# Forming the low half of each weight block by an accumulating DMA

## The chip, the cores and the metric

The kernel runs on one core of one Trainium2 chip. The metric is the device time of one execution in microseconds (us). Before the change it is 972.54 us, the median of three runs (970.15 to 978.56).

## What is computed

Two layers act on x, 512 rows of 1024 float32 numbers. Each is x + rmsnorm(mixer(rmsnorm(x))). The even layer has one input projection, which feeds an S5 state-space branch and a convolution branch, and one output projection. The odd layer is a chunked gated linear attention (GLA) with four heads. Cut to the parts that matter here:

```python
u = rms_norm(x, norm_pre[0]);  p = u @ ev_w_in[0]
a_in, a_z, b_val, b_gate, b_z = split(p)
ya = gelu(s5_layer(a_in, ...))                       # 64 groups, 64 complex states each
ya = ya * sigmoid(ya @ s5_w_glu + s5_b_glu) * silu(a_z)
yb = silu(layer_norm(causal_depthwise_conv31(b_val * sigmoid(b_gate)))) @ conv_w_pw * silu(b_z)
x = x + rms_norm(concat(ya, yb) @ ev_w_out[0], norm_post[0])
u = rms_norm(x, norm_pre[1]);  q, k, v, r, lr = split(u @ od_w_in[0])
y = rms_norm(gla_chunked(q, k, v, log_sigmoid(lr @ w_gate_up + b) / 16)) * silu(r)
x = x + rms_norm(y @ od_w_out[0], norm_post[1])
```

## The kernel before

**Two halves of every matrix.** TensorE (PE) multiplies in a rounded 32-bit format (fp32r). To keep float32 accuracy, activations and weights are each split in two: a high half, which is the rounded value, and a low half, which is the value less the rounded one. A product is the sum of three matmuls: high weight by high activation, high weight by low activation, low weight by high activation.

**136 weight blocks in a row.** All weights form one list (`wlist`, L87 to L112) of blocks of 128 x 1024 numbers, 512 KB each: 40 of the input projection, 8 of the GLU, 8 of the S5 half of the output projection, 8 of the pointwise projection, 8 of the convolution half, then for each of four heads 12 blocks (queries and keys, values, gate), with 8 blocks of the second output projection after the heads 2 and 3. `w_raw` (L115) starts the load of a block into one of three `wraw` buffers from SyncE's (SP's) DMA queue. `w_split` (L124) turns it into `wh` and `wl`, with two buffers each: ScalarE (ACT) makes the rounded copy at L138, and VectorE (DVE) or GpSimd (POOL) subtracts it from the raw block at L140. The set `pool_split` (L151) gives 45 blocks to POOL and leaves the rest to DVE. `w_get` (L156) hands over the next block and splits the one after it. The instructions of `w_split` are recorded under `feed()` (L145), a higher priority for the scheduler. Ten blocks are split into resident tiles instead, `hres`/`lres` at the end of each output projection (L865 to L868) and `wres` (L940); these are not split ahead.

**How a block is used.** `mm_st` (L170) uses the weights as the stationary operand: 16 matmuls with `wh` (L175, L176), then 8 with `wl` (L178). It serves 72 blocks. `mm_mv` (L765) streams the weights as the moving operand, and L773, L774 (with `wh`) and L775 (with `wl`) take turns, so that `wl` is needed from the first matmuls on. It serves the 32 blocks of values and gates and the 32 of the output projections; ten of these 64 are the resident ones.

**What else is in the queues.** While the 40 blocks of the input projection are multiplied, the S5 branch runs for eight channel tiles c: `s5_prep` makes tables (DVE and POOL), `s5_in` a scan over blocks of time (L563 to L589, mostly DVE), `s5_out` the outputs (PE). The convolution (`conv`, L622) has 31 taps of 128x512 for each tile, the first on ACT (L625) and 30 on DVE (L628, L629), recorded under `background()`, a low priority. After it come GLU, layer norm and the two halves of the output projection; then the heads of layer 1. A scheduler orders the instructions of each engine when the kernel is built, and each engine then runs its own queue in that order and waits at the head of it. The DMA instructions of an engine stand in the same queue.

## Time and profile before

| | |
|---|---|
| runs | 970.15, 972.54, 978.56 us |
| profiled execution: span from first to last instruction | 977.0 us, 4.5 us (0.5%) above the median; what the execution takes outside its span is shown by no view |
| PE busy | 910.5 us (93%) |
| DVE busy | 722.4 us (74%), over 98% of the time from 50 to 400 us |
| ACT busy | 430.9 us (44%) |
| POOL busy | 403.9 us (41%), most of it before 250 us |
| DMA | 109.17 MB, all issued from SP; its queue took 32.8% of the sixteen engines |
| PE clock, mean over the span | 0.978 of full |

In the lines of the profile, L140 is line 140 of the kernel before; `x12` counts instructions; "busy, mean ns" is their time together and of one; "idle before <-releaser" is what the engine waited for ahead of them. In a table of windows each engine has its busy time in the stretch and in brackets its instructions, PEclk is the clock that PE was granted, and "DMA share" is the mean busy share of the sixteen DMA engines. A chain shows the work that ended last, step by step.

### The profile page before, as it was taken

Reading aid. Unit: us, or ns where it says so; the run is one execution under the profiler, and the core shown is the slowest. Engines: PE = TensorE matmul, PEld = TensorE weight load, DVE = VectorE, ACT = ScalarE, POOL = GpSimd, SP = SyncE. Lnnn points to the kernel's source line nnn. Section 1 sums busy time; section 2 is a strip of 40 time slices with the busy share of each in tenths; the row PEclk is TensorE's granted clock in tenths of the full one; section 3 lists DMA queues with packets and bytes.
Section 4 is the critical chain, followed back from the end, with each engine's and each line's share of the span. In section 5 each row is a group of like instructions: output and inputs, shape, how many; then the busy total and the mean of one; then the engine's idle time right before and its main releaser. Section 6 shows DMA issues by size and latency. Waiting matters only on the chain.

```text
span 977.0 us, 11973 instructions
## 1 busy us (share of the span) xinstructions
PE 910.5 (93%) x4396; PEld 726.1 (74%) x4396; DVE 722.4 (74%) x1210; ACT 430.9 (44%) x646; POOL 403.9 (41%) x335
## 2 busy tenths in 40 slices
PE   4978998699799999999999898999999999999996
PEld 3866776476577777777888676788888888888875
DVE  7999999999999999894457758857374322563546
ACT  5313566565454843454244465434353342342431
POOL 3499999999833594751126203100020020000212
PEclk9998999889899999999999999999999999999998
DMA  6333423334324433415244311311212123323612
GB/s 216 130 102 110 144 65 121 101 100 121 100 79 140 162 112 126 161 66 172 87 162 155 136 58 50 130 66 65 82 70 87 65 87 129 129 83 138 232 44 86
DMA packets 44330, 109.17 MB, mean 112 GB/s; under 512 B 12849, under 2 KB 14385, under 8 KB 44273
## 3 DMA queue, kind: packets, MB, share of 16 engines
q1 hardware_dynamic: 44272, 108.42, 32.8%
q8 instruction: 34, 0.56, 0.2%
q14 instruction: 24, 0.19, 0.1%
HBM read 95.18 MB, written 13.22 MB: 111 GB/s over the span
## 4 chain that ended last, share of the span: by engine, by line
PE 51%; DVE 25%; ACT 4%; issue 2%; DMA 1%; POOL 0%; DVEq 0%; SPq 0%; ACTq 0%; POOLq 0%
DVE ps_cv L628 8%; PE ps_mm L773 8%; PE ps_mm L775 8%; PE ps_mm L774 8%; PE ps_mm L178 6%; PE ps_mm L175 6%; PE ps_mm L176 6%; PE ps_aux L1035 2%; DVE zb L580 1%; DVE cme L484 1%; DVE cme L488 1%; PE ps_mm L880 1%; PE ps_mm L876 1%; PE ps_mm L877 1%; DVE bcum L955 1%
## 5 line engine op out<-in xcount | busy, mean ns | idle before, releaser
L138 ACT CAST wh<-wraw 128x1024 fp32r<-128x1024 f32 x125 | 131.3, 1050 | 177.2 <-PE ps_mm L774 81.1
L140 DVE TENSOR_TENSOR wl<-wraw,wh 128x1024 fp32r<-128x1024 f32 x82 | 108.1, 1319 | 101.2 <-ACT wh L138 99.4
L628 DVE SCALAR_TENSOR_TENSOR ps_cv<-h,cw,ps_cv 128x512 f32<-128x512 f32 x232 | 162.0, 746 | 1.9 <-ACT ps_cv L625 0.9
L140 POOL TENSOR_TENSOR wl<-wraw,wh 128x1024 fp32r<-128x1024 f32 x44 | 112.1, 2548 | 106.4 <-ACT wh L138 61.0
L175 PE MATMUL ps_mm<-u0h,wh 128*128 128x512 f32 x320 | 133.3, 417 | 8.4 <-ACT tmp L652 8.4
L176 PE MATMUL ps_mm<-u0l,wh 128*128 128x512 f32 x320 | 130.8, 409 | 0.0
L773 PE MATMUL ps_mm<-wh,u1h 128*128 128x512 f32 x240 | 95.1, 397 | 0.2 <-DVE bcum L948 0.2
L774 PE MATMUL ps_mm<-wh,u1l 128*128 128x512 f32 x240 | 94.8, 395 | 0.0
L775 PE MATMUL ps_mm<-wl,u1h 128*128 128x512 f32 x240 | 90.7, 395 | 0.0
L178 PE MATMUL ps_mm<-u0h,wl 128*128 128x512 f32 x320 | 85.1, 403 | 5.2 <-DVE wl L140 5.2
L175 PEld LDWEIGHTS ps_mm<-u0h,wh 128*128 128x128 f32 x320 | 63.1, 197 | 26.6 <-ACT tmp L652 10.1
L178 PEld LDWEIGHTS ps_mm<-u0h,wl 128*128 128x128 f32 x320 | 59.8, 191 | 20.6 <-DVE wl L140 6.1
L176 PEld LDWEIGHTS ps_mm<-u0l,wh 128*128 128x128 f32 x320 | 62.9, 197 | 14.5 <-issue 1.0
L935 POOL TENSOR_TENSOR rg<-rg,ng 128x512 f32<-128x512 f32 x16 | 25.5, 1626 | 114.8 <-ACT rg L934 114.8
L1021 POOL TENSOR_TENSOR kr<-kr,fac 128x384 f32<-128x384 f32 x8 | 8.4, 1044 | 136.9 <-DVE rs_y L189 77.7
L773 PEld LDWEIGHTS ps_mm<-wh,u1h 128*128 128x128 f32 x240 | 45.2, 188 | 10.7 <-DVE bcum L948 0.5
L774 PEld LDWEIGHTS ps_mm<-wh,u1l 128*128 128x128 f32 x240 | 45.2, 188 | 10.0
L775 PEld LDWEIGHTS ps_mm<-wl,u1h 128*128 128x128 f32 x240 | 45.0, 188 | 10.2
L176 PE MATMUL ps_mm<-u1l,wh 128*128 128x512 f32 x128 | 50.7, 396 | 0.0
L175 PE MATMUL ps_mm<-u1h,wh 128*128 128x512 f32 x128 | 50.6, 395 | 0.0
L178 PE MATMUL ps_mm<-u1h,wl 128*128 128x512 f32 x128 | 35.1, 412 | 3.4 <-DVE wl L140 3.4
L773 PE MATMUL ps_mm<-wh,oth 128*128 128x512 f32 x96 | 38.0, 397 | 0.1
(356 smaller groups left out, 2134.3 us busy)
## 6 DMA issues: line engine op xcount, KB each, us to landing
wraw<-in_w_in_dram SPq DMA_DIRECT2D x40, 512.0 KB, 3.3
wraw<-in_w_out_dram SPq DMA_DIRECT2D x32, 512.0 KB, 3.3
wraw<-in_w_vr_dram SPq DMA_DIRECT2D x32, 512.0 KB, 3.2
wraw<-in_w_qk_dram SPq DMA_DIRECT2D x16, 512.0 KB, 3.2
tm<-kt_d SPq DMA_DIRECT2D x8, 512.0 KB, 4.6
wraw<-in_w_glu_dram SPq DMA_DIRECT2D x8, 512.0 KB, 3.6
wraw<-in_w_pw_dram SPq DMA_DIRECT2D x8, 512.0 KB, 3.2
x<-in_x_dram SPq DMA_DIRECT2D x4, 512.0 KB, 5.2
```

What stands on the lines that cost most here:

```text
L138: SC.copy(h, raw)
L140: eng.tensor_tensor(out=l, in0=raw, in1=h.bitcast(F32), op=ALU.subtract)
L175: PE.matmul(acc, whv[:, k, :], xh[:, k, :], start=(k == 0), stop=False)
L176: PE.matmul(acc, whv[:, k, :], xl[:, k, :], start=False, stop=False)
L178: PE.matmul(acc, wlv[:, k, :], xh[:, k, :], start=False, stop=(k == KT - 1))
L484: eng.tensor_tensor(out=o, in0=pr[:, 0, hg, lo:lo + TB].unsqueeze(pa).to_broadcast(sh), in1=m1.unsqueeze(5 - pa).to_broadcast(sh), op=ALU. ...
L628: V.scalar_tensor_tensor(out=acc, in0=h[:, k:k + S], scalar=cw[:, c, k:k + 1], in1=acc, op0=ALU.mult, op1=ALU.add)
L773: PE.matmul(accs[tt], xh[:, kt, ts_], whj, start=(first and j == 0), stop=False)
L774: PE.matmul(accs[tt], xl[:, kt, ts_], whj, start=False, stop=False)
L775: PE.matmul(accs[tt], xh[:, kt, ts_], wlj, start=False, stop=(last and j == 1))
L935: G.tensor_tensor(out=r_, in0=r_, in1=ng, op=ALU.mult)
L1035: PE.matmul(acc[:, 0:n], a[:, j, k0:k0 + P], b[:, j, q0:q0 + n], start=st_, stop=sp_)
```

## The change

The subtraction goes. For every block, ACT writes the negated rounded block into the `wl` buffer (an activation with scale -1), and POOL issues a DMA that adds the raw block, on chip, onto what stands there: -rounded(w) + w is the low half. The DMA moves `wraw` to `wl` with an accumulating write. `wl` gets a third buffer, and the negation and the DMA of block i+1 are recorded right behind the split of block i, one block earlier than the rounded copy of i+1; blocks in resident tiles, and the block behind one, have no such lead. `pool_split` is gone, and all blocks go this way. The cast of block 78, which was on DVE, goes to ACT.

```diff
+    def w_low(i, dst=None):
+        while wst["next_raw"] <= i:
+            w_raw()
+        l = wpool.tile([P, 1024], F32R, tag="wl", bufs=3, name=f"wl{i}") if dst is None else dst
+        raw = wst["raw"][i]
+        with feed():
+            SC.activation(l, raw, AF.Copy, scale=-1.0)
+            G.dma_start(l.bitcast(F32), raw, accum_op=ALU.add)
+        wst["low"][i] = l
+
     def w_split(dst=None):
         i = wst["next_split"]
         while wst["next_raw"] <= i:
             w_raw()
+        if i in dma_low and i not in wst["low"]:
+            w_low(i, dst and dst[1])
         raw = wst["raw"].pop(i)
-        if dst is None:
-            h = wpool.tile([P, 1024], F32R, tag="wh", bufs=2, name=f"wh{i}")
-            l = wpool.tile([P, 1024], F32R, tag="wl", bufs=2, name=f"wl{i}")
+        h = wpool.tile([P, 1024], F32R, tag="wh", bufs=2, name=f"wh{i}") if dst is None else dst[0]
+        with feed():
+            SC.copy(h, raw)
+        if i in dma_low:
+            l = wst["low"].pop(i)
         else:
-            h, l = dst
-        with feed():
-            if i in {78}:
-                V.tensor_copy(h, raw)
-            else:
-                SC.copy(h, raw)
-            eng = G if i in pool_split else V
-            eng.tensor_tensor(out=l, in0=raw, in1=h.bitcast(F32), op=ALU.subtract)
...
         w_raw()
+        if i + 1 in dma_low and i + 1 not in w_resident and i not in w_resident:
+            w_low(i + 1)
...
-    pool_split = {0, 1} | set(range(18, 56)) | {57, 60, 63, 66, 69}
+    dma_low = set(range(len(wlist)))
...
-        za, zb, zc = (h5.tile([P, S], F32, tag=n, bufs=b, name=f"{n}{c}") for n, b in (("za", 1), ("zb", 2), ("zc", 2)))
+        za, zb, zc = (h5.tile([P, S], F32, tag=n, bufs=b, name=f"{n}{c}") for n, b in (("za", 1), ("zb", 1), ("zc", 1)))
```

The room for the third buffer comes from elsewhere. `zb` and `zc` of the S5 scan have one buffer in place of two (above). `ones` and `cw` move to the pool that is closed after the convolution branch; `reset` and `mask` are made at the start of layer 1; some tiles of a few bytes have two buffers in place of four.

The line numbers shift by 5 to 13: L138 becomes L143, L628 becomes L641. The scheduler orders the queues anew. In the rows below each row is an instruction, output <- inputs, in the order of its engine's queue.

DVE, in the input projection, at the scan of the second S5 channel tile (`za`, `zb`, `zc`, `sv`) and the convolutions of the first two tiles (`ps_cv`). Before:

```order
L576 TENSOR_TENSOR za_1000<-za_1000,zb_1001 128x512
L140 TENSOR_TENSOR wl_1499<-wraw_1403,wh_1498 128x1024
L653 TENSOR_TENSOR h_1461<-ps_mm,tmp 128x512
L628 SCALAR_TENSOR_TENSOR ps_cv<-h_1148,cw,ps_cv 128x512
L580 SCALAR_TENSOR_TENSOR zb_1001<-zc_1002,za_1000 128x512
L628 SCALAR_TENSOR_TENSOR ps_cv<-h_1148,cw,ps_cv 128x512
```

The change, at the scan of the first tile, where the write of the second `h` stands now:

```order
L589 TENSOR_TENSOR za_934<-za_934,zb_935 128x512
L641 SCALAR_TENSOR_TENSOR ps_cv<-h_1162,cw,ps_cv 128x512
L593 SCALAR_TENSOR_TENSOR zb_935<-zc_936,za_934 128x512
L641 SCALAR_TENSOR_TENSOR ps_cv<-h_1162,cw,ps_cv 128x512
L666 TENSOR_TENSOR h_1479<-ps_mm,tmp 128x512
L641 SCALAR_TENSOR_TENSOR ps_cv<-h_1162,cw,ps_cv 128x512 x2
```

The subtraction between the steps of the scan is gone from DVE; the convolution fills the places. Counted over the queue, 154 rows of the convolution's L628 stood ahead of the last `sv` before, and 161 of L641 now.

POOL, in the same stage, at the tables of S5 channel tile 4 (`pt_4`, `bmt`). Before:

```order
L486 TENSOR_TENSOR pt_4_1665<-pr,bb_1584 128x512
L479 TENSOR_TENSOR bb_1897<-bb_1897,bt_1898 128x128
L140 TENSOR_TENSOR wl_1744<-wraw_1536,wh_1743 128x1024
L585 MEMSET sv_1639 128x8
L484 TENSOR_TENSOR bmt_1664<-pr,bb_1584 128x512
L488 TENSOR_TENSOR bmt_1664<-bmt_1664,pt_4_1665 128x512
```

The change:

```order
L131 DMA wl_1837<-wraw_1766 128x1024
L499 TENSOR_TENSOR pt_4_1685<-pr,bb_1604 128x512
L492 TENSOR_TENSOR bb_1921<-bb_1921,bt_1922 128x128
L598 MEMSET sv_1659 128x8
L497 TENSOR_TENSOR bmt_1684<-pr,bb_1604 128x512
L501 TENSOR_TENSOR bmt_1684<-bmt_1684,pt_4_1685 128x512
```

A DMA instruction stands where a subtraction stood, in front of the same table work.

ACT, at the gate of head 1 in layer 1 (`rg` is the gate's output). Before:

```order
L138 CAST wh_5956<-wraw_5900 128x1024
L138 CAST wh_5986<-wraw_5930 128x1024
L934 ACT_TABLE_LOAD
L934 ACTIVATE rg_6016<-ps_mm 128x512
L934 ACTIVATE rg_6019<-ps_mm 128x512
L934 ACTIVATE rg_6022<-ps_mm 128x512
L138 CAST wh_6171<-wraw_5960 128x1024
```

The change:

```order
L143 CAST wh_6085<-wraw_6025 128x1024
L130 ACTIVATE wl_6089<-wraw_6056 128x1024
L947 ACT_TABLE_LOAD
L947 ACTIVATE rg_6116<-ps_mm 128x512
L947 ACTIVATE rg_6119<-ps_mm 128x512
L947 ACTIVATE rg_6122<-ps_mm 128x512
L143 CAST wh_6271<-wraw_6056 128x1024
L130 ACTIVATE wl_6275<-wraw_6087 128x1024
```

Behind every rounded copy stands the negation of the next block; wraw_6056 is read first by the negation and, one step later, by its rounded copy.

More of the change, by code (lines that the diff above doesn't have):

```diff
@@ L112, in trunk @@
                     wlist.append(A["w_out1"][n, (h - 2) * 4 + j])
-    wst = {"next_raw": 0, "next_split": 0, "raw": {}, "hl": {}}
+    wst = {"next_raw": 0, "next_split": 0, "raw": {}, "hl": {}, "low": {}}
     def w_raw():
@@ L127, in w_split @@
             w_raw()
+        if i in dma_low and i not in wst["low"]:
+            w_low(i, dst and dst[1])
         raw = wst["raw"].pop(i)
-        if dst is None:
-            h = wpool.tile([P, 1024], F32R, tag="wh", bufs=2, name=f"wh{i}")
-            l = wpool.tile([P, 1024], F32R, tag="wl", bufs=2, name=f"wl{i}")
-        else:
-            h, l = dst
-        with feed():
-            if i in {78}:
-                V.tensor_copy(h, raw)
-            else:
-                SC.copy(h, raw)
-            eng = G if i in pool_split else V
-            eng.tensor_tensor(out=l, in0=raw, in1=h.bitcast(F32), op=ALU.subtract)
+        h = wpool.tile([P, 1024], F32R, tag="wh", bufs=2, name=f"wh{i}") if dst is None else dst[0]
[3 more added lines that the diff above has]
+            l = wst["low"].pop(i)
+        else:
+            l = wpool.tile([P, 1024], F32R, tag="wl", bufs=3, name=f"wl{i}") if dst is None else dst[1]
+            with feed():
+                V.tensor_tensor(out=l, in0=raw, in1=h.bitcast(F32), op=ALU.subtract)
         wst["hl"][i] = (h, l)
@@ L205, in sumsq @@
             junk = tmp((P, D), mybir.dt.bfloat16, "junk")
-        ss = small.tile([P, 1], F32, tag=tag, name="ss")
+        ss = small.tile([P, 1], F32, tag=tag, bufs=2 if tag == "ss1" else 4, name="ss")
         SC.activation(junk[:, :n], src, AF.Square, accum_out=ss)
@@ L241, in bigt @@
         return big.tile([P, KT, S], dt, tag="big", name=name)
+    ones = hpool.tile([P, P], F32, tag="ones", bufs=1, name="ones")
+    G.memset(ones, 1.0 / D)
     uh = bigt(F32R, "u0h")
@@ L914, in trunk @@
     SY.dma_start(ng, A["gla_g"].partition_broadcast(P))
+    reset = pa.tile([P, S], mybir.dt.bfloat16, name="reset")
+    G.memset(reset, 1.0)
+    G.memset(reset.rearrange("p (c t) -> p c t", t=64)[:, :, 0:1], 0.0)
+    mask = pa.tile([P, 2, 64], I32, name="mask")
+    mf = tmp((P, 2, 64))
+    G.memset(mf, 1.0)
+    G.affine_select(out=mf[:, 0, :], in_=mf[:, 0, :], pattern=[[1, 64]], compare_op=ALU.is_ge, fill=0.0, base=0, channel_multiplier=-1)
+    G.affine_select(out=mf[:, 1, :], in_=mf[:, 1, :], pattern=[[1, 64]], compare_op=ALU.is_ge, fill=0.0, base=64, channel_multiplier=-1)
+    G.memset(mf[0:64, 1, :], 0.0)
+    V.tensor_copy(mask, mf)
     PG = ExitStack()
@@ L1017, in trunk @@
             V.tensor_mul(kr[:, 0:S], acc, en[j])
-            fac = small.tile([P, 3, 2], F32, tag="fac", name=f"fac{h}{j}")
+            fac = small.tile([P, 3, 2], F32, tag="fac", bufs=2, name=f"fac{h}{j}")
             V.tensor_copy(fac[:, :, 0], es[:, 0:3])
```

20 lines of the change are left out of this document (4 added, 16 removed).

## The prediction

> **What bounds the kernel now.** I read busy time by stretches first, then the chain in the stretch where PE is not full.
>
> ```profile
> core 0: us, PE busy (x) PEld busy (x) DVE busy (x) ACT busy (x) POOL busy (x), PEclk, DMA share, GB/s
> 50.00:316.00 266.00, 232.00 (x1361) 178.05 (x1360) 262.62 (x302) 130.31 (x205) 223.77 (x190) 0.94 0.34 108
> 316.00:400.00 84.00, 81.12 (x374) 64.36 (x373) 83.49 (x110) 43.74 (x56) 53.41 (x27) 1.00 0.40 135
> 400.00:950.00 550.00, 540.99 (x2431) 438.49 (x2430) 317.88 (x613) 231.17 (x345) 99.89 (x63) 0.99 0.31 106
> 950.00:977.00 27.00, 18.63 (x83) 15.05 (x81) 16.87 (x45) 3.61 (x10) 6.43 (x5) 0.91 0.21 78
> ```
>
> From 50 to 316 us (S5 branch and most of the input projection) DVE is busy 262.6 of 266 us, POOL 223.8, while PE has 34 us idle and a clock of 0.94, which costs it up to another 16. From 316 to 950 PE is busy 622 of 634 us. The chain from 150 to 316 us, by line:
>
> ```profile
> by line: DVE ps_cv L628 43.4%; DVE zb L580 7.9%; DVE cme L484 6.9%; DVE cme L488 6.6%; DVE pt L486 5.2%; issue 4.5%; DVE za L576 4.0%; DVE zb L575 3.7%; DVE sv L588 3.0%; DVE zb L583 2.2%; DVE zc L584 2.2%; DVE za L574 2.1%; DVE h L629 1.6%
> ```
>
> So the first stretch goes at DVE's pace and the rest at PE's. Work taken off DVE counts in full only before 316 us; afterwards it counts only where PE waited for it.
>
> **What the subtractions cost there.** DVE's and POOL's rows of L140 by stretch, and the groups that take most of DVE's time beside them (50 to 400 us):
>
> ```profile
> core 0: us, DVE busy (x) POOL busy (x), PEclk, DMA share, GB/s
> 50.00:316.00 266.00, 21.48 (x12) 44.79 (x18) 0.94 0.34 108
> 316.00:400.00 84.00, 0.00 (x0) 33.26 (x13) 1.00 0.40 135
> 500.00:950.00 450.00, 87.41 (x68) 4.82 (x2) 1.00 0.29 103
> ```
>
> ```profile
> L484 DVE TENSOR_TENSOR cme<-pr,csp 128x512 f32<-128x512 f32 x16 | 20.2, 1299 | 0.0
> L488 DVE TENSOR_TENSOR cme<-cme,pt 128x512 f32<-128x512 f32 x16 | 19.8, 1239 | 0.0
> L580 DVE TENSOR_TENSOR_SCAN zb<-zc,za 128x512 f32<-128x512 f32 x8 | 17.4, 2177 | 0.0
> L486 DVE TENSOR_TENSOR pt<-pr,ci 128x512 f32<-128x512 f32 x16 | 17.0, 1064 | 0.1
> L574 DVE TENSOR_TENSOR za<-ps_aux,ct 128x512 f32<-128x512 f32 x8 | 5.4, 681 | 0.0
> ```
>
> The same lines by shortest, median and longest:
>
> ```profile
> L484 DVE TENSOR_TENSOR cme<-pr,csp x16: 679/1522/1773, 55.2 to 245.1; 128x512 f32<-128x512 f32 x16
> L580 DVE TENSOR_TENSOR_SCAN zb<-zc,za x8: 1211/2106/3093, 118.9 to 312.2; 128x512 f32<-128x512 f32 x8
> ```
>
> L574, with one input in PSUM, always takes its 681 ns. The others have both inputs in SBUF: L484 can take 679 too, but its median is 1522. Two rows of the timeline, POOL's and DVE's, show why:
>
> ```profile
> 188.30 2.37 POOL L140 TENSOR_TENSOR wl<-wraw,wh 128x1024 fp32r<-128x1024 f32 x1
> ```
>
> ```profile
> 188.66 3.09 DVE L580 TENSOR_TENSOR_SCAN zb<-zc,za 128x512 f32<-128x512 f32 x1
> ```
>
> POOL's subtraction ends at 190.67; the scan, begun 0.36 us after it, ends 1.08 us after that, about its shortest time of 1.21. DVE waited the POOL instruction out. The Trainium skill (SBUF — State Buffer, Who interferes with whom) says so: a DVE instruction with two SBUF inputs contends with a GpSimd instruction that reads SBUF, not with one that only writes; by that a DMA instruction on POOL would not block these rows.
>
> **The sum, 50 to 316 us.** Off DVE: 12 subtractions, 21.5 us. From contention: the four slow groups lose 16 x (1.299-0.679) = 9.9, 16 x 0.56 = 9.0, 8 x (2.177-1.211) = 7.7 and 16 x 0.385 = 6.2, in all 32.8 us, and the smaller groups of the kind perhaps 20 more. Subtractions are 44.8 of POOL's 223.8 us, a fifth, but an instruction that waits for a POOL one of 2.4 us waits longer than for one of 1.3; I give them a quarter of some 50, 12 us (bounds 0 and 17). Back come 7 rows of the convolution that now stand ahead of the last scan, 7 x 0.746 = 5 us. Net 21.5 + 12 - 5 = 28.5 us. PE would allow 34 + 16 = 50, so it does not cap this. But some of PE's waits there end with ACT:
>
> ```profile
> PE ps_aux L601 <- ACT bm L505: 8.0, 3, 3.6
> PE ps_mm L175 <- ACT tmp L652: 7.9, 3, 5.6
> PE ps_aux L503 <- ACT kt L516: 5.3, 1, 5.3
> ```
>
> ACT gets about 29 negations there at the price of its cast, 30 us on 130 of 266: not full, but each can stand ahead of such a row. I count three quarters of 28.5: **21 us gained** (bounds 0, and 28.5 + 5 = 34).
>
> **316 us and after.** From 316 to 400 us DVE is as full as PE (83.5 against 81.1 of 84): it must end the convolution before the layer norm. Of its 83.5 the 5 us of convolution have gone forward, and 33 us of POOL's subtractions no longer block its rows, so it should need less than PE's 81 and the 21 us are kept. Then PE is the bound, and the 87.4 us off DVE from 500 to 950 are worth only the waits of PE for a low half:
>
> ```profile
> PE ps_mm L178 <- DVE wl L140: 3.4, 2, 2.4
> PE ps_mm L775 <- DVE wres L140: 1.6, 1, 1.6
> PE ps_mm L775 <- POOL wl L140: 0.4, 1, 0.4
> ```
>
> That is 5.4 us at most. Against it stand the resident blocks, whose negation has no lead: in place of 1.22 us of DVE their low half takes a negation and a DMA. I set 3 us for `wres` and 2 for the last projection, where `hres` and `lres` now hold their raw buffers longer. These cancel. The 143 us of negations on ACT (136 x 1.05) are hidden as long as PE's next low half is not late.
>
> **When is it late?** The prices, from the rows of the casts and the subtractions, SP's issue, the landings and the queue:
>
> ```profile
> L138 ACT CAST wh<-wraw 128x1024 fp32r<-128x1024 f32 x125 | 131.3, 1050 | 177.2 <-PE ps_mm L774 81.1
> L140 POOL TENSOR_TENSOR wl<-wraw,wh 128x1024 fp32r<-128x1024 f32 x44 | 112.1, 2548 | 106.4 <-ACT wh L138 61.0
> L120 SPq DMA_DIRECT2D wraw<-in_w_in_dram x40: 327/328/659, 3.2 to 324.1; - x40
> wraw<-in_w_in_dram SPq DMA_DIRECT2D x40, 512.0 KB, 3.3
> xr<-x_d SPq DMA_DIRECT2D x4, 512.0 KB, 10.9
> q1 hardware_dynamic: 44272, 108.42, 32.8%
> ```
>
> PE's pace, by the starts of two successive groups of `wl` matmuls when it waits for nothing:
>
> ```profile
> 468.00 2.03 PE L178 MATMUL ps_mm<-xbh,wl 128*128 128x512 f32 x8
> 473.59 2.02 PE L178 MATMUL ps_mm<-xbh,wl 128*128 128x512 f32 x8
> ```
>
> A block takes 5.59 us. In `mm_mv` a `wl` buffer is held for a whole block; then ACT makes the cast (1.05) and the negation (1.05), then the DMA takes D from the end of the negation to its landing. With three buffers, 1.05 + 1.05 + D + 5.59 must fit into 3 x 5.59 = 16.8: D up to 9.1 us is hidden. `mm_st` needs `wl` 16 matmuls later and leaves 3.7 us more. No row shows an accumulating DMA or any DMA from POOL. Its issue lies between SP's 0.33 and the subtraction's 2.5; its landing between a load of the same size, 3.3, and the slowest 512 KB row, 10.9. Since it reads two blocks and writes one, I take twice a load, 6.6, and an issue of 1.4: **D = 8.0** (bounds 3.6 and 13.4), hidden with 1.1 us to spare. On POOL, 1.4 is less than the 2.5 it replaces. At the upper bound, 13.4, a block takes (2.1 + 13.4 + 5.59)/3 = 7.03 and the 54 streamed blocks of `mm_mv` lose up to 78 us.
>
> So the forecast is 977.0 - 21 = 956 for the profiled execution. That lies 4.5 us above the median of the runs, and against the median it is 972.5 - 21 = **952 us**, own range 938 to 962.
>
> **Rivals.** *Nothing gained early.* DVE's queue empties faster, but S5 goes through ACT between its steps, and ACT's in-order queue with 29 more instructions keeps PE waiting: 21.2 us of waits on ACT are there already (above), and `zb`, `zc` now have one buffer. For it: those rows; against: they are a small part beside a DVE that is 98.7% full. Then a quarter of 28.5 stays, and a few us go at the resident blocks: about 968.
>
> *The low half is late (the slower side).* D exceeds 9.1 us in the dense `mm_mv` stretches: value, gate and output projections, L775. At D = 12 a block takes (2.1 + 12 + 5.59)/3 = 6.56, 0.97 more; times 54 blocks 52 us, less the 21 gained: 1004. It turns the result negative from 54 x (D - 9.1)/3 = 21, D = 10.3. For it: my 8.0 leaves little, POOL's queue also holds table work, and loads share the sixteen engines; against: 3.3 us is what 512 KB takes now, and the heads have attention matmuls between blocks. The Trainium skill names another way to a large D (SBUF — State Buffer, SBUF: two separate sides): while DVE runs certain one-input SBUF instructions, GpSimd cannot write its DMA descriptors; its section on who interferes has 620 ns become 3100. Such rows of DVE in the heads are short:
>
> ```profile
> L1006 DVE TENSOR_SCALAR qr<-qr,ec 128x64 f32<-128x64 f32 x32 | 6.1, 249 | 0.0
> L1009 DVE TENSOR_SCALAR qr<-qr,es 128x128 f32<-128x128 f32 x8 | 2.3, 282 | 0.0
> ```
>
> If a DMA on POOL had to wait out one or two of them, D would be 8.0 + 0.6 = 8.6, still under 9.1: as a mechanism of its own this has 0.03 of the 0.20 below, and only where several follow each other.
>
> *DMA engines full.* 32.8% of 977 us for 108.42 MB is 1.55 us of all sixteen for 512 KB. Twice that for the accumulation makes 4.65 of 5.59 us in a dense stretch: tight, but it fits. If accumulating runs at a quarter of the load's rate, 1.55 + 6.2 = 7.75, 2.2 us more on up to 96 blocks (136 less the 40 of the slow first stretch), 208 us, half of it absorbed by attention, less the gain: about 1060. The Trainium skill (Collectives: The Full Stack, The bandwidth ceiling) has the add itself free and the second read halve the rate; by that, the 4.65 holds.
>
> **How the numbers follow.** A measurement of this kernel tells about 1% from no change: 963 to 982 is the same. Chances: forecast 0.52, nothing gained early 0.20, late low half 0.20, DMA engines full 0.08. So faster 0.52, same 0.20, slower 0.28. The range is 937 to 1006: below it lies what is left of 34 us gained with later waits gone too, above it the DMA rival and half of the late one.
>
> **What would show it.** Right: DVE's groups L497, L501, L499 (L484, L488, L486 before) near 0.9 us in place of 1.1 to 1.3; the last S5 scan 20 us earlier; PE above 622 of 634 us from there to the tail; DMA landings from POOL of 6 to 8 us; the DMA share from 0.33 to about 0.76 (136 x 3.1 us on 977 more). Wrong: PE waits at the lines of `wl` ended by a DMA, in sum over 20 us; or the stretch of the S5 branch as long as before with PE waiting for ACT; or a DMA share over 0.9 in dense stretches.

## The result, and the profile after

The changed kernel takes 987.72 us (median of four runs, 986.97 to 988.38) against 972.12 us for the kernel before (four runs, 970.15 to 978.56). The ratio on record is 1.0141, 95% interval 1.0112 to 1.0171 (the two medians alone make 1.016): slower by 1.4%, where 952 us was forecast. The profiled execution of the changed kernel has a span of 986.6 us, the one before 977.0. The latter lies above its median, so the profiles compared below show 9.6 us of a loss that is 15.6 between the medians.

The stretches of the prediction, now for the changed kernel (busy time of each engine, granted clock, DMA share, GB/s):

```profile
50.00:316.00 266.00, 233.17 (x1387) 177.85 (x1387) 242.20 (x297) 166.86 (x245) 173.91 (x195) 0.94 0.68 171
316.00:400.00 84.00, 79.61 (x356) 63.30 (x353) 73.66 (x105) 55.23 (x71) 35.03 (x33) 1.00 0.89 231
400.00:950.00 550.00, 528.33 (x2361) 426.09 (x2360) 199.85 (x516) 300.59 (x409) 124.73 (x130) 0.99 0.73 183
```

VectorE (DVE, the third figure) is no longer full before 316 us: 242.2 of 266, where it had 262.6. What was bought there is paid back later: from 400 to 950 us PE has lost 12.7 us (541.0 to 528.3). The last column but one shows what else has changed: the DMA engines are 0.68 to 0.89 busy where they were 0.31 to 0.40.

The places of the loss are seen by the end of the last matmul of each piece of work on PE's timeline (us; the columns beside are experiments told below):

| last matmul of | before | changed | rooms only | blocks 0 to 55 only | from 56 only | resident by DVE | traffic only | eighth | early, from DRAM |
|---|---|---|---|---|---|---|---|---|---|
| input projection (`u0h`) | 349.3 | 339.9 | 342.8 | 337.1 | 346.4 | 338.2 | 337.7 | 338.5 | 331.9 |
| pointwise projection (`xbh`) | 492.3 | 481.4 | 489.9 | 478.8 | 489.2 | 479.8 | 479.9 | 480.2 | 469.6 |
| streamed half of `ybh` | 514.6 | 510.6 | 512.4 | 501.3 | 519.1 | 504.2 | 502.4 | 502.7 | 492.0 |
| resident half of `ybh` | 537.3 | 542.5 | 535.1 | 524.0 | 550.5 | 531.7 | 524.2 | 527.0 | 514.8 |
| transposes of `xg` | 555.7 | 566.7 | 552.7 | 541.6 | 573.8 | 550.5 | 557.5 | 551.3 | 532.4 |
| gates (`gws`) | 579.1 | 585.7 | 576.1 | 565.0 | 592.8 | 573.9 | 576.5 | 570.3 | 555.8 |
| last values and gates (`u1h`) | 915.9 | 920.7 | 914.1 | 904.6 | 927.9 | 909.0 | 916.1 | 905.4 | 894.6 |
| resident half of `oth` | 968.6 | 978.2 | 967.3 | 957.9 | 985.4 | 970.5 | 971.7 | 958.9 | 948.1 |

The changed kernel is 10.9 us ahead at the end of `xbh` and 6.6 behind at the end of `gws`: 17.5 us lost at the end of layer 0. In the heads it gains 1.8 back, and in the last projection it loses another 4.8. Between those two places it is no slower. The first of them in one row each, the changed kernel, then the one before:

```profile
481.40:585.70 104.30, 90.64 (x372) 70.01 (x372) 44.29 (x107) 50.24 (x80) 32.07 (x31) 0.93 0.70 179
```

```profile
492.30:579.10 86.80, 83.56 (x373) 66.38 (x372) 59.19 (x118) 38.55 (x67) 27.46 (x18) 1.00 0.38 130
```

The same matmuls (372 and 373 in the records). PE is idle for 13.7 us instead of 3.2, which is 10.4 of the 17.5, and busy for 90.6 instead of 83.6, the other 7.1: the granted clock is 0.93 there, and 0.83 and 0.70 in the ten microseconds from 490 and from 530 us, in which PE waited most. Of the 13.7 us, 5.1 end with the DMA of a low half (`wl`, `wres`, `lres`), 3.4 with ACT's cast of a rounded half, 4.4 with the normalised rows `xg`. In the changed kernel as a whole PE's waits for these are:

```profile
PE ps_mm L189 <- DMA wl<-wraw: 10.6, 6, 3.6
...
PE ps_mm L786 <- ACT wh L143: 6.1, 3, 3.1
PE ps_aux L236 <- DVE xg L232: 4.4, 1, 4.4
...
PE ps_mm L788 <- DMA wres<-wraw: 2.5, 1, 2.5
PE ps_mm L186 <- ACT wh L143: 2.5, 2, 1.6
```

Both places by DMA share, first the changed kernel (the columns as above):

```profile
440.00:490.00 50.00, 50.00 (x219) 40.89 (x218) 11.46 (x16) 20.75 (x24) 6.92 (x8) 1.00 0.91 219
490.00:500.00 10.00, 6.94 (x24) 5.16 (x23) 2.00 (x4) 6.27 (x10) 1.72 (x2) 0.83 0.61 147
500.00:530.00 30.00, 26.98 (x115) 20.89 (x114) 9.56 (x16) 13.70 (x21) 12.98 (x11) 1.00 0.95 232
910.00:930.00 20.00, 20.00 (x90) 16.22 (x90) 4.94 (x16) 9.15 (x14) 6.77 (x6) 1.00 1.01 323
930.00:950.00 20.00, 17.08 (x75) 12.55 (x74) 6.02 (x20) 12.38 (x17) 4.31 (x5) 1.00 0.93 236
```

and the kernel before:

```profile
500.00:530.00 30.00, 30.00 (x132) 24.53 (x132) 19.95 (x29) 12.20 (x21) 15.97 (x9) 1.00 0.50 175
910.00:930.00 20.00, 20.00 (x93) 16.32 (x92) 13.40 (x31) 11.38 (x18) 6.04 (x4) 1.00 0.44 162
```

Where weights stream at PE's full pace the share is 0.91, with nothing lost yet (50.00 of 50). Where the resident blocks, the gains and the rows of the residual come on top, it is 0.93 to 1.01 in three of the rows, and PE falls back in two of them. The share alone does not say when: from 910 to 930 us it is 1.01 and PE is still full, and in the ten microseconds in which PE waits most, from 490 and from 530, it is 0.61 and 0.62. The chain of waits from 470 us on, the larger pieces that are DMAs and negations up to 513 us, shows what PE waits for (start, length, what):

```profile
477.27 7.80 DMA wl<-wraw
485.13 5.17 DMA wraw<-in_w_out_dram
490.32 1.06 ACT lres L130
...
496.89 8.30 DMA wl<-wraw
505.24 6.39 DMA wraw<-in_w_out_dram
511.65 1.06 ACT lres L130
```

An accumulating DMA holds its raw buffer until it lands; only then can SyncE load the next block into it, and only then can ScalarE (ACT) negate that. ScalarE's longest waits for a DMA, from 440 to 570 us, are for exactly those loads:

```profile
ACT lres L130 <- DMA wraw<-in_w_out_dram: 17.6, 3, 7.3
...
ACT wl L130 <- DMA wraw<-in_w_vr_dram: 9.9, 1, 9.9
```

What stands behind such a negation in ScalarE's queue waits too. ScalarE is idle for 7.34 us until the negation of 490.32; the cast of the streamed block that PE needs next comes behind the resident block's own cast and six small ones, at 494.59, and PE stands from 492.6 to 495.7 for it.

The queues and the landings of the changed kernel (median us from issue to landing):

```profile
q0 software_dynamic: 19584, 71.31, 39.6%
q1 hardware_dynamic: 44272, 108.42, 32.5%
```

```profile
wl<-wraw POOLq DMA_DIRECT2D x126, 512.0 KB, 5.7
wraw<-in_w_out_dram SPq DMA_DIRECT2D x32, 512.0 KB, 4.9
...
xr<-x_d SPq DMA_DIRECT2D x4, 512.0 KB, 17.8
```

39.6% of 986.6 us for 136 accumulating DMAs is 2.87 us of all sixteen engines each (3.1 forecast), and the median landing of 5.7 us lies below the 8.0 forecast. Neither price was too low; the two, 2.87 and the load's 1.55, make 4.4 us of a block's 5.59, 0.79. The rows of the residual, `xr<-x_d`, went from 10.9 to 17.8.

### The profile page after: what moved, and what is told of

Its sections match the earlier page's. It is cut to its first block, busy times and chain, and to the rows that moved or that the text cites. A ratio compares the mean times of both kernels' runs of the same rounds, so it can differ in the third digit from the quotient of the medians.

```text
span 986.6 us, 12310 instructions
## 1 busy us (share of the span) xinstructions
PE 910.2 (92%) x4396; PEld 723.3 (73%) x4396; DVE 578.2 (59%) x1118; ACT 558.3 (57%) x781; POOL 370.1 (38%) x426
## 3 DMA queue, kind: packets, MB, share of 16 engines
q0 software_dynamic: 19584, 71.31, 39.6%
## 4 chain that ended last, share of the span: by engine, by line
PE 49%; DVE 24%; DMA 12%; issue 5%; ACT 5%; POOL 3%; SPq 0%; DVEq 0%; POOLq 0%; ACTq 0%
PE ps_mm L787 8%; PE ps_mm L788 8%; PE ps_mm L786 8%; DVE ps_cv L641 6%; DMA wl<-wraw 5%; PE ps_mm L189 5%; PE ps_mm L186 5%; PE ps_mm L187 5%; DMA wraw<-in_w_out_dram 3%; DVE cme L497 2%; PE ps_aux L1048 2%; DVE cme L501 2%; DMA cb<-in_s5cb_dram 1%; DVE pt L499 1%; DVE bcum L968 1%
## 5 line engine op out<-in xcount | busy, mean ns | idle before, releaser
L131 POOL DMA_DIRECT2D wl<-wraw x126 | 112.1, 892 | 441.8 <-ACT wl L130 383.9
L143 ACT CAST wh<-wraw 128x1024 fp32r<-128x1024 f32 x126 | 132.0, 1048 | 116.7 <-PE ps_mm L787 58.4
L641 DVE SCALAR_TENSOR_TENSOR ps_cv<-h,cw,ps_cv 128x512 f32<-128x512 f32 x232 | 162.9, 747 | 2.7 <-ACT ps_cv L638 1.4
L130 ACT ACTIVATE wl<-wraw 128x1024 fp32r<-128x1024 f32 x126 | 133.2, 1057 | 46.7 <-PE ps_mm L189 11.1
L186 PE MATMUL ps_mm<-u0h,wh 128*128 128x512 f32 x320 | 129.9, 407 | 2.4 <-ACT tmp L665 1.8
L187 PE MATMUL ps_mm<-u0l,wh 128*128 128x512 f32 x320 | 128.1, 401 | 0.0
L788 PE MATMUL ps_mm<-wl,u1h 128*128 128x512 f32 x240 | 94.4, 398 | 0.0
L189 PE MATMUL ps_mm<-u0h,wl 128*128 128x512 f32 x320 | 86.4, 407 | 6.2 <-DMA wl<-wraw 6.2
L189 PEld LDWEIGHTS ps_mm<-u0h,wl 128*128 128x128 f32 x320 | 60.4, 193 | 22.1 <-DMA wl<-wraw 7.9
L187 PEld LDWEIGHTS ps_mm<-u0l,wh 128*128 128x128 f32 x320 | 61.5, 192 | 14.1 <-issue 1.3
L786 PEld LDWEIGHTS ps_mm<-wh,u1h 128*128 128x128 f32 x240 | 45.4, 189 | 13.0 <-ACT wh L143 2.2
L788 PEld LDWEIGHTS ps_mm<-wl,u1h 128*128 128x128 f32 x240 | 45.5, 190 | 10.8
L787 PEld LDWEIGHTS ps_mm<-wh,u1l 128*128 128x128 f32 x240 | 45.5, 190 | 10.4
L209 DVE TENSOR_SCALAR vv<-ss 128x1 f32<-128x1 f32 x32 | 4.8, 150 | 81.5 <-ACT tmp L1092 66.4
L787 PE MATMUL ps_mm<-wh,otl 128*128 128x512 f32 x96 | 38.0, 396 | 0.0
L788 PE MATMUL ps_mm<-wl,oth 128*128 128x512 f32 x96 | 37.3, 395 | 0.1
```

Of the source, the lines that this page charges most:

```text
L130: SC.activation(l, raw, AF.Copy, scale=-1.0)
L131: G.dma_start(l.bitcast(F32), raw, accum_op=ALU.add)
L143: SC.copy(h, raw)
L186: PE.matmul(acc, whv[:, k, :], xh[:, k, :], start=(k == 0), stop=False)
L187: PE.matmul(acc, whv[:, k, :], xl[:, k, :], start=False, stop=False)
L189: PE.matmul(acc, wlv[:, k, :], xh[:, k, :], start=False, stop=(k == KT - 1))
```

## The experiments

All are edits of the changed kernel. Chips differ by up to 0.5% in the kernel before (971.7 to 976.3 us), so versions from different batches are compared by their ratio to the kernel before on the same chip.

**Resident blocks by VectorE.**

```diff
-    dma_low = set(range(len(wlist)))
+    dma_low = set(range(len(wlist))) - (set(range(68, 72)) | {74, 75} | set(range(len(wlist) - 4, len(wlist))))
```

> The changed kernel with the ten resident blocks (68 to 71, 74, 75 and the last four) taken back to VectorE's subtraction; the other 126 still get their low half by the accumulating DMA. Theory A: the loss sits where the low half has no lead, at the resident blocks: negation, accumulating DMA and reload of the raw buffer stand one behind another there (chain of 475 to 545 us: 7.80, 5.17, 8.30, 6.39, 6.26, 4.05 us). Then the stretch from the last matmul on xbh to the last transpose of xg, 86.0 us after the change and 64.2 before, falls to 64 to 70, the last projection gains some 4 us more, and the whole run comes to about 965 us (960 to 970). Rival B: the streamed blocks beside them are late too, since every raw buffer is held until its DMA lands: half of the loss at most comes back, 975 to 982. Rival C: DMA engines or ScalarE are simply too full everywhere: nothing comes back, 985 or more.

Measured: 978.67 us, ratio 1.0054 (1.002 to 1.0089). About 9 us come back, not 22: theory A falls and rival B holds. The table shows that the stretch from `xbh` to `xg` is 70.7 us (85.3 in the changed kernel, 63.4 before), but that the last projection still loses, 61.5 us from `u1h` to the end of `oth` against 52.7 before, though all its resident blocks are VectorE's again.

**Blocks 0 to 55 only.**

```diff
+    dma_low = set(range(56))
```

> The accumulating DMA for blocks 0 to 55 alone (S5 branch, value and gate, GLU, first half of the output projection); from block 56 on VectorE subtracts. Theory A and rival B both: the lead of 9 to 11 us that the changed kernel has at the last matmul on xbh (479.6 against 490.3) stays to the end, about 962 us (957 to 967). Rival C (the gain by 480 us is no gain, or the new buffers cost later): 970 or more.

Measured: 966.77 us, ratio 0.9917 (0.9885 to 0.9948), as A and B had it. The lead of 13.5 us at `xbh` is 10.7 at the end.

**From block 56 only.** Blocks 0 to 55 are split as in the kernel before.

```diff
+    dma_low = set(range(56, len(wlist)))
+    pool_split = {0, 1} | set(range(18, 56)) | {57, 60, 63, 66, 69}
...
-                V.tensor_tensor(out=l, in0=raw, in1=h.bitcast(F32), op=ALU.subtract)
+                (G if i in pool_split else V).tensor_tensor(out=l, in0=raw, in1=h.bitcast(F32), op=ALU.subtract)
```

> The accumulating DMA from block 56 on alone; blocks 0 to 55 are split as in the kernel before (GpSimd for 0, 1 and 18 to 55, VectorE for the rest). Theories A and B: no lead is built, and the 22 us of 480 to 565 us and 5 us at the end are lost, part of it given back in the heads: about 990 us (985 to 997). If the loss came from the early part, 975 or less.

Measured: 995.99 us, ratio 1.0218 (1.0179 to 1.0257). The loss needs no early part.

**The rooms alone.** As the one above with `dma_low = set()`, and block 78's rounded half on VectorE as before.

> No accumulating DMA at all: every low half by GpSimd or VectorE as in the kernel before, but in the changed kernel's rooms (three low buffers, zb and zc and other small tiles with fewer buffers, constants made elsewhere). If the rooms are free, 972 us as before (968 to 976). If the single zb and zc hold back the S5 branch, as one of the rivals of the prediction had it, 978 to 985, and the lost 11 of the 21 us forecast for that branch are explained by them; the last S5 scan then starts later than 312 us.

Measured: 974.23 us, ratio 1.0008 (0.9984 to 1.0031). Fewer buffers for `zb`, `zc` and the small tiles cost nothing that can be measured. These four ran on one chip, so they add up: against the rooms alone the early part is worth 974.2 - 966.8 = 7.5 us, the late part costs 996.0 - 974.2 = 21.8, and their sum, 14.3, is the changed kernel's 987.7 - 974.2 = 13.5 within 1 us (its chip and this one have the kernel before at 972.1 and 971.7). By the table the changed kernel is 2.9 us ahead of the rooms alone at `u0h` and 8.5 at `xbh`, the one with blocks 0 to 55 alone 5.7 and 11.1: half of the gain or more comes after the input projection.

**The second input from DRAM.** The raw buffer is free once ScalarE has read it.

```diff
-            G.dma_start(l.bitcast(F32), raw, accum_op=ALU.add)
+            G.dma_start(l, wlist[i].bitcast(F32R), accum_op=ALU.add)
```

> The changed kernel, but the accumulating DMA takes the weight block from DRAM a second time in place of the raw buffer, so the raw buffer is free as soon as ScalarE has read it twice and nothing else of the order is changed on purpose. Theory A2 (raw supply): the three raw buffers are held until the DMA lands (5 to 9 us), so loads start late, ScalarE stands in its queue at a negation whose block isn't there (8.1 us at 931.7) and what stands behind it waits. Then most of the 22 us of 480 to 565 us and of the 10 us at the end comes back: 958 to 972. Rival D (the low half itself lands too late, or the DMA engines are full): the second read costs as much or more on the engines and the landing is no earlier: 985 or more.

Measured: 979.3 us, ratio 1.0039 (1.0013 to 1.0065). Ten us come back, less than A2 asked and more than D allows. Most of that was earned before 480 us (the end of `xbh` at 473.9 against 481.4); from `xbh` to `gws` it took 100.5 us against 104.3, and 86.8 before. So the held buffer counts, above all early, but the late loss as a whole does not hang on it: with free raw buffers it is nearly as large. It stands elsewhere, though: from `xbh` to the end of the resident `ybh` this kernel takes 52.7 us (61.1 in the changed kernel, 45.0 before), so half of that loss is gone, and from there to `gws` 47.8 (43.2 and 41.8).

**Four raw and two low buffers.**

```diff
-        raw = wpool.tile([P, 1024], F32, tag="wraw", bufs=3, name=f"wraw{i}")
+        raw = wpool.tile([P, 1024], F32, tag="wraw", bufs=4, name=f"wraw{i}")
...
-        l = wpool.tile([P, 1024], F32R, tag="wl", bufs=3, name=f"wl{i}") if dst is None else dst
+        l = wpool.tile([P, 1024], F32R, tag="wl", bufs=2, name=f"wl{i}") if dst is None else dst
```

> The changed kernel with four raw buffers and two low buffers in place of three and three (the same room). Theory A2: the added raw buffer is worth more than the low one: faster than the changed kernel's 987.7, 970 to 982. Rival D (low half late): with two low buffers a block must fit its negation, DMA and matmuls, 1.05 + 1.05 + 5.7 + 5.59 = 13.4 us, into 11.2: the dense stretches lose up to 2.2 us a block, 1000 us or more.

Measured: 1021.07 us, ratio 1.0463 (1.0419 to 1.0507); A2 wrong, D's number right. PE's longest wait by far in that kernel:

```profile
PE ps_mm L788 <- DMA wl<-wraw: 34.0, 19, 6.0
```

With two low buffers the landing is no longer hidden; with three the same wait is 1.3 us in the changed kernel. The third buffer was needed, in line with the prediction's 16.8 us.

**The DMA in the heads, not at the layer ends.**

```diff
+    dma_low = set(range(56)) | set(range(76, 124))
```

> The accumulating DMA for blocks 0 to 55 and 76 to 123 (all but the two output projections' ends and the first blocks of layer 1); VectorE subtracts for 56 to 75 and 124 to 135. Theory A2: the DMA costs only where raw blocks are needed faster than they come back; in the heads it does not cost, so this is as fast as the one with blocks 0 to 55 alone (966.8) or 1 to 3 us faster, 962 to 968. If the streamed blocks of the heads lose too: 970 or more.

Measured: 968.34 us, ratio 0.993 (0.9903 to 0.9958), the same as with blocks 0 to 55 alone. 48 more blocks by DMA cost nothing in the heads, where the engines' share is 0.67 (580 to 900 us), and gain nothing that can be measured.

**Ports and DMAs by themselves.** Loops of eight VectorE and GpSimd (POOL) instructions, then single and grouped DMAs, each group begun when all before it is done.

```diff
+    for _ in range(8):
+        V.tensor_tensor(out=va, in0=va, in1=vb, op=ALU.mult)
+    for _ in range(8):
+        G.tensor_tensor(out=ga, in0=ga, in1=gb, op=ALU.mult)
...
+    for i in range(4):
+        G.dma_start(lows[i], raws[i], accum_op=ALU.add)
+        SY.dma_start(lds[i], A["w_pw"][i])
```

> A measurement by itself; nothing of the reference is computed, the output is zero. (1) Eight VectorE adds of two SBUF inputs, 128x512, alone; (2) the like beside eight GpSimd instructions back to back; (3) the same with a DMA issue after each second GpSimd instruction; (4) with one input in PSUM beside a string of eight. Theory P: a VectorE instruction with two SBUF inputs that meets a string of GpSimd instructions waits until the string ends, not just until one instruction ends: in (2) one of them takes as long as what is left of the string, 5 to 10 us, in (3) at most 3 to 4 us, in (1) and (4) all near 0.68 us. Rival: each waits for one GpSimd instruction, 1.0 to 1.5 us apiece in (2) and no difference in (3). (5) to (9): accumulating DMAs alone, loads alone, four accumulating DMAs at once, four beside four loads, four with the second input from DRAM. Theory A2 needs 5 us or more for one alone and 8 or more beside loads; the forecast's D was 8.0, and its share of sixteen engines 3.1 us each.

Measured, VectorE beside the string of group (2), and the landings of (5), one accumulating DMA alone, of (6), one load alone, and of (8), the accumulating DMAs when four of each start at once, and last the two queues:

```profile
L90 DVE TENSOR_TENSOR va<-va,vb x8: 691/1632/1636, 24.6 to 35.4; 128x512 f32<-128x512 f32 x8
```

```profile
DMA to landing us min/median/max: 4.5/4.5/4.6
```

```profile
DMA to landing us min/median/max: 3.0/3.2/3.3
```

```profile
DMA to landing us min/median/max: 8.2/13.2/16.6
```

```profile
q0 software_dynamic: 2880, 10.49, 27.1%
q1 hardware_dynamic: 2304, 8.39, 11.2%
```

Twenty accumulating DMAs take 27.1% of 202.4 us, 2.74 us of all sixteen engines each, sixteen loads and stores 1.42 each. Four accumulations make 4 x 2.74 = 11.0 us, and in (7) the last landed after 10.9; four of both make 4 x (2.74 + 1.42) = 16.6, and the last landed after 16.6. So the times on the engines add, whichever of the two queues they come from. With the second input from DRAM, (9), the last of four landed after 11.0: no dearer. Theory P falls: each VectorE instruction waited for one GpSimd instruction, 1.63 us, not for the string.

**Traffic only.** The kernel with blocks 0 to 55 by DMA, and from block 56 on two writes of each low block to DRAM that nothing reads.

```diff
                 V.tensor_tensor(out=l, in0=raw, in1=h.bitcast(F32), op=ALU.subtract)
+                if i >= 56:
+                    for n in range(2):
+                        G.dma_start(spare[(2 * i + n) % 8], l.bitcast(F32))
```

> The kernel with the accumulating DMA for blocks 0 to 55 alone (966.8), and from block 56 on, where VectorE subtracts, two DMAs from GpSimd's queue write each finished low block to spare DRAM. Nothing reads them and no raw buffer, negation or low half waits for them; they only load the sixteen DMA engines about as an accumulating DMA does (1.42 us of all sixteen for one load, 2.74 for one accumulation, by the measurement alone). Theory A3 (the DMA engines are full where weights stream at full pace and other 512 KB transfers come between, so raw blocks arrive late: share 0.88 to 1.04 in 440 to 490, 500 to 530 and 910 to 930 us against 0.2 to 0.65 before): this alone loses 10 to 20 us at the two layer ends, 977 to 987. Rival A2 (raw buffers held by the DMA, negations queued on ScalarE): none of that is here, so 966 to 971.

Measured: 982.05 us, ratio 1.0077 (1.005 to 1.0104), against 0.9917 without the writes (on another chip): 1.6%, 15.5 us, for transfers for which no negation, no raw block and no low half waits. The queue of GpSimd and the stretch in which PE falls back most, then the chain there:

```profile
q0 software_dynamic: 31104, 113.26, 37.3%
```

```profile
530.00:540.00 10.00, 6.34 (x23) 4.50 (x23) 4.97 (x19) 2.94 (x5) 3.38 (x3) 0.80 1.00 378
```

```profile
531.50 10.04 DMA xr<-in_x_dram
```

The 160 writes add 37.3% of 982.1 less 16.5% of 966.3, 207 us: 2.59 us of all engines a block, a little less than an accumulation. A row of the residual, whose loads land in 4.9 us without the traffic, takes 10.04 and the normalisation waits for it. So a full set of DMA engines can cost as much as this, but the place is another than in the changed kernel. There the streamed and resident blocks lose 16.1 us, from the end of `xbh` to that of the resident `ybh`, and what follows them to `gws` 1.4; here what follows them loses 11.3 against the kernel without the writes, and the streamed and resident blocks lose nothing:

```profile
479.90:524.20 44.30, 44.30 (x194) 35.97 (x194) 28.38 (x49) 17.84 (x32) 20.82 (x26) 1.00 0.94 363
```

At a share of 0.94 PE is busy all the time there. Full engines by themselves do not make the 16.1 us; something must also wait for the accumulation.

**The negation on GpSimd, from block 56 on.**

```diff
-            SC.activation(l, raw, AF.Copy, scale=-1.0)
+            if i >= 56:
+                G.tensor_scalar(out=l, in0=raw, scalar1=-1.0, scalar2=None, op0=ALU.mult)
+            else:
+                SC.activation(l, raw, AF.Copy, scale=-1.0)
```

> The changed kernel with the negation of blocks 56 and later on GpSimd in place of ScalarE. If what costs is ScalarE's in-order queue (a negation that waits 8.1 us for its raw block at 931.7 us with the head's output rows behind it), the loss after the heads, 4.8 us, and a good part of the 22 us at 480 to 565 come back: 965 to 978. If the DMA engines are the bound (A3), little changes: 982 to 992, a GpSimd negation taking about 2.4 us against 1.05.

Measured: 1010.09 us, ratio 1.0356 (1.0317 to 1.0396): slower than either had it. Two rows, GpSimd's negation and PE's longest wait:

```profile
L131 POOL TENSOR_SCALAR wl<-wraw 128x1024 fp32r<-128x1024 f32 x70 | 200.1, 2861 | 157.3 <-PE ps_mm L791 101.1 <-PE ps_mm L192 39.1 <-DMA wraw<-in_w_vr_dram 8.5
```

```profile
PE ps_aux L239 <- DVE xg L235: 19.2, 2, 12.0
```

At 2.86 us it stands before the multiplications of the normalisation on GpSimd, and PE waits there. The time as a whole does not support ScalarE's queue as the cause, but the streamed and resident blocks do: from `xbh` (476.7) to the resident `ybh` (522.1) this kernel takes 45.4 us, where the changed kernel takes 61.1 and the one before 45.0. That is a hint and no proof, since fewer bytes pass in it (180 GB/s over 45.4 us, 203 over 61.1) and the loss follows behind.

**Half and an eighth of the bytes, from block 56 on.** The rest of each low block stays the negated block, so part of the low products is left out; every instruction and wait stays.

```diff
-            G.dma_start(l.bitcast(F32), raw, accum_op=ALU.add)
+            n = 1024 if i < 56 else 512
+            G.dma_start(l[:, 0:n].bitcast(F32), raw[:, 0:n], accum_op=ALU.add)
```

> The changed kernel, but from block 56 on the accumulating DMA moves only the first 512 of 1024 columns; the other half of each low block stays the negated block, so that part of the computation is left out. Negations, DMA issues, buffers and waits are all as in the changed kernel; only the bytes are fewer. Theory A3 (bytes on the DMA engines, 1.42 + 2.85 of 5.59 us a block at full pace): with 1.42 + 1.4 the engines are half full and most of the loss is gone: 966 to 974. Rival A4 (the chain itself: negation without lead on ScalarE, GpSimd's issue, a raw buffer held by one more step): the landing gets shorter by some 1 us only, so 978 to 986.

> The same with the first 128 columns only from block 56 on. A3: nothing left of the loss, 963 to 970, as with the DMA for blocks 0 to 55 alone. A4: 976 to 984.

Measured: 972.46 us, ratio 0.9972 (0.9942 to 1.0002), for the half; 968.16 us, ratio 0.9929 (0.9902 to 0.9956), for the eighth (128 columns). Full, half, eighth and none: 1.0141, 0.9972, 0.9929, 0.9917. The 80 negations on ScalarE, the 80 issues on GpSimd, the resident blocks without a lead are all still there in the eighth and in sum cost nothing that can be measured (by the profiles it loses 3.9 us against blocks 0 to 55 alone from `xbh` to `gws`, and gains 4.5 in the heads). The dense stretch of above in it, and its landing:

```profile
440.00:490.00 50.00, 50.00 (x219) 40.87 (x218) 13.55 (x20) 27.52 (x35) 8.46 (x10) 1.00 0.47 137
```

```profile
wl<-wraw POOLq DMA_DIRECT2D x70, 64.0 KB, 2.5
```

A4 falls: the loss goes with the bytes of the accumulating DMA. What these two don't part is a full engine from a longer landing, since fewer bytes shorten both (5.7 to 2.5 us). The traffic alone parts them only so far: it costs 15.5 us, but none of them where the changed kernel loses 16.1.

**The best of both.**

```diff
-            G.dma_start(l.bitcast(F32), raw, accum_op=ALU.add)
+            G.dma_start(l, wlist[i].bitcast(F32R), accum_op=ALU.add)
...
-    dma_low = set(range(len(wlist)))
+    dma_low = set(range(56)) | set(range(76, 124))
```

> Accumulating DMA for blocks 0 to 55 and 76 to 123 only, with the second input read from DRAM, so that raw buffers are freed early; VectorE subtracts the others. The run with all blocks from DRAM was 18.4 us ahead of the kernel before at the last matmul on xbh and lost it afterwards at blocks that are left out here. All theories: faster than the kernel before; 953 to 963 us, and not slower than the 966.8 and 968.3 of the two kernels that read the raw buffer.

Measured: 964.3 us, ratio 0.9898 (0.9863 to 0.9932), hardly better than with the raw buffer.

The same for blocks 0 to 55 alone, `dma_low = set(range(56))`:

> The accumulating DMA for blocks 0 to 55 alone, its second input read from DRAM so that the raw buffer is free early; VectorE subtracts the rest. If raw buffers held by the DMA cost in the first stretch too, 1 to 5 us faster than the 966.8 of the same with the raw buffer (a ratio of 0.987 to 0.991 in place of 0.992); if not, the same.

Measured: 959.01 us (958.58 to 959.93), ratio 0.9847 (0.9795 to 0.9898): 16 us faster than the kernel before on that chip, 2.9% faster than the changed kernel by the ratios. Its stretches:

```profile
50.00:316.00 266.00, 239.89 (x1435) 184.19 (x1434) 253.51 (x310) 170.46 (x249) 173.07 (x195) 0.96 0.70 176
316.00:400.00 84.00, 83.22 (x355) 66.15 (x354) 71.88 (x101) 54.26 (x70) 36.96 (x33) 1.00 0.89 237
400.00:950.00 550.00, 538.03 (x2433) 437.12 (x2431) 306.02 (x629) 229.24 (x344) 70.58 (x56) 1.00 0.31 107
```

Early DMA share as in the changed kernel, late DMA share as before: the gain without the loss. By its profile it is 17.4 us ahead at `u0h`, 5 more than with the raw buffer held; the intervals of the two (0.9795 to 0.9898, 0.9885 to 0.9948) overlap, so the 5 us are not shown. The kernel before this one treats blocks 0 to 55 in the same way and ends `u0h` at 336.6 us, not 331.9, so the scheduler's order or chance can move as much.

**Strings of independent GpSimd instructions.** What VectorE does beside GpSimd instructions that don't need one another.

```diff
+    for _ in range(12):
+        V.tensor_tensor(out=va, in0=va, in1=vb, op=ALU.add)
+    for i in range(8):
+        G.tensor_tensor(out=outs[i], in0=ga, in1=gb, op=ALU.mult)
```

> A measurement by itself; nothing of the reference is computed, the output is zero. Twelve VectorE instructions with two SBUF inputs, 128x512, beside GpSimd instructions: (1) eight, each on the result of the one before, (2) eight that don't need one another, (3) eight with accumulating DMAs, (4) two that don't need one another. In the earlier measurement, with dependent GpSimd instructions, VectorE's took 1.63 us each, at most 2.61, so it got one in after each. Theory Q: instructions of GpSimd that don't need one another run on without a gap, and VectorE waits for the whole string: in (2) one VectorE instruction of 8 us or more and eleven of 0.69. Rival: 1.6 us each in (2) as in (1); then the 7.31 and 9.84 us of the changed kernel have another cause.

Measured for (2):

```profile
L93 DVE TENSOR_TENSOR va<-va,vb x12: 691/1632/1635, 35.1 to 50.7; 128x512 f32<-128x512 f32 x12
```

Theory Q falls too: again one after one, 1.63 us, and the twelve take 15.8 us in (1), (2) and (3) alike.

## Why the prediction was wrong, step by step

**The step that failed** is the one after 316 us: the 5 us set for the resident blocks against 5.4 us of saved waits ("These cancel"), the negations "hidden as long as PE's next low half is not late", and the engines' "4.65 of 5.59 us in a dense stretch: tight, but it fits". Measured: the DMA from block 56 on costs 21.8 us where zero was forecast. Of the 5 us none was set for the resident blocks at the end of layer 0, where most is lost; with all ten back on VectorE some 9 us return. The price was right (2.87 us, 4.4 with the load). But the budget held weights only: at the two layer ends the residual, its stores, the gains and `yp` use the same engines, and landings and loads of raw blocks grow longer. And the condition for the negations looked at the low half alone: a negation that waits for its raw block also holds up the casts behind it, and after 316 us PE waits 8.6 us for rounded halves, where it waited 0.3 before.

What is shown: the loss needs the bytes of the accumulating DMA, since an eighth of them, with every instruction and wait in place, costs nothing in sum; and bytes alone are not enough where most is lost, since traffic that nothing waits for costs nothing there. What was traced, and not tested by itself, is the way between: accumulation, raw buffer, load, negation at the head of ScalarE's queue, cast, PE. A raw buffer freed early halves the loss from `xbh` to the resident `ybh`. How the 21.8 us divide between the links, and how much is the load of the residual behind full engines, is open.

**The early gain** had the right sign and a third of the size: 7.5 us (early part against rooms alone) for 21. The 21.5 us of subtractions did leave VectorE (17.6 in the kernel with the rooms alone). Its busy time from 50 to 316 us fell by the same 17.6 against that kernel (259.8 to 242.2), and it stood idle instead: 23.8 us, 10.4 of them waiting for ACT's `tmp` (L665) and 8.0 for PE. The term that failed is "from contention", 12 us. VectorE's groups in the changed kernel, 50 to 316 us:

```profile
L501 DVE TENSOR_TENSOR cme<-cme,pt 128x512 f32<-128x512 f32 x16 | 22.7, 1418 | 0.0
L497 DVE TENSOR_TENSOR cme<-pr,csp 128x512 f32<-128x512 f32 x14 | 21.2, 1549 | 0.0
L499 DVE TENSOR_TENSOR pt<-pr,ci 128x512 f32<-128x512 f32 x15 | 20.0, 1334 | 2.8 <-ACT ci L482 2.3 <-DVE cme L501 0.5
L593 DVE TENSOR_TENSOR_SCAN zb<-zc,za 128x512 f32<-128x512 f32 x8 | 14.3, 1784 | 0.0
```

and in the one with the rooms alone:

```profile
L498 DVE TENSOR_TENSOR cme<-pr,csp 128x512 f32<-128x512 f32 x16 | 18.8, 1216 | 0.0
L502 DVE TENSOR_TENSOR cme<-cme,pt 128x512 f32<-128x512 f32 x16 | 18.7, 1167 | 0.0
...
L500 DVE TENSOR_TENSOR pt<-pr,ci 128x512 f32<-128x512 f32 x16 | 17.5, 1092 | 0.1
L594 DVE TENSOR_TENSOR_SCAN zb<-zc,za 128x512 f32<-128x512 f32 x8 | 13.3, 1667 | 1.2 <-POOL zc L593 1.2
```

Over the shortest times of the prediction (679 ns, and 1211 for the scan) that is 16 x 0.739 + 14 x 0.870 + 15 x 0.655 + 8 x 0.573 = 38.4 us against 16 x 0.537 + 16 x 0.488 + 16 x 0.413 + 8 x 0.456 = 26.7: 12 us more, not 12 less (6 more than the 32.8 of the kernel before). Five smaller groups with two inputs in SBUF (L588, L589, L596, L597, L601) fell together from 45.6 to 38.0, so that in sum there is no relief, but 4 us more than with the rooms alone. The excess comes from few instructions: three of the 45 rows shown for `cme` and `pt` took 8.75, 7.31 and 5.43 us, 19.4 of the 38.4, where the longest with the rooms alone took 2.82. The median fell or stayed (0.69, 1.02 and 1.02 us in the order above, 1.04, 0.99 and 1.03 there). One of the three:

```profile
202.87 7.31 DVE L501 TENSOR_TENSOR cme<-cme,pt 128x512 f32<-128x512 f32 x1
```

It ends at 210.2, when GpSimd, which had worked without a gap since 202.5, is through (last row 208.99 + 0.62). Why such an instruction is kept out for a whole string is open: two measurements by themselves gave one GpSimd instruction's wait each time. That GpSimd's table work stands closer together without the subtractions is likely, and not shown to be the cause. The prediction cited the Trainium skill (SBUF — State Buffer, Who interferes with whom), that a DVE instruction with two SBUF inputs contends with a GpSimd instruction that reads SBUF; the measurement agrees: 1.63 us beside GpSimd with two inputs in SBUF, and with one input in PSUM, of which the next line is, 0.70.

```profile
L105 DVE TENSOR_TENSOR acc<-acc,vb x8: 699/699/699, 66.0 to 71.1; 128x512 f32<-128x512 f32 x8
```

What was wrong was to count the relief by the share of the removed instructions, as if the rest would block as before.

**D**, forecast 8.0 us (3.6 to 13.4): from issue to landing 4.5 alone, 5.7 at the median and up to 10.4 in the changed kernel. With three buffers little of it shows in the `mm_mv` stretches (1.3 us at L788); with two (and four raw buffers) PE waits 34 us there.

**The rivals.** "The low half is late" by a D over 10.3 us is not what happened: after 316 us PE's waits that end with a low half's DMA sum to 9.5 us in the changed kernel (`wl` 4.4 at L189 and 1.3 at L788, `wres` 2.5, `lres` 1.3), where 5.4 ended with a subtraction before. These 4 us more are part of the loss, not most of it. The other way to a large D, GpSimd kept from its descriptors, did not show: an issue took 0.86 us at the median and 1.69 at most. (The 620 and 3100 ns that the prediction names with it stand in another section of that page of the Trainium skill: SBUF — State Buffer, A bandwidth-pool intuition that's wrong.) "DMA engines full" named a part of the cause with a chance of 0.08 and a wrong condition: it asked for an accumulation at a quarter of the load's rate, when the ordinary rate suffices once other transfers share the stretch and the next negation waits for them. That the accumulation costs about twice a load, as the prediction took it, agrees: 2.74 us of the engines against 1.42. "Nothing gained early" kept a quarter of 28.5 us, and 7.5 is what came, which is luck: its single `zb` and `zc` are refuted by the rooms alone, and PE's waits for ACT, 21.2 us before, are 8.6 from 50 to 316 us in the changed kernel; it is VectorE that waits for ACT now.

**The signs.** VectorE's groups near 0.9 us: no, 1.3 to 1.5. Last scan 20 us earlier: 8 (312.2 to 304.1), and none of it by the DMA, since with the rooms alone it starts at 304.2. PE over 622 of 634 us from 316: 607.9. Landings of 6 to 8 us: 5.7. Share 0.76: 0.72. Of the signs named for being wrong, "a DMA share over 0.9 in dense stretches" showed; PE's waits at the lines of `wl` that end with a DMA are 15.7 us over the whole run, under its 20.
